# Output projection of a hybrid decoder block with seven products for eight, over pairs of token tiles

## The chip, the cores and the metric

The kernel runs on one core of a Trainium2 chip. The metric is the device time of one execution in microseconds. A core has TensorE (matmuls into the accumulators, PSUM), VectorE, ScalarE and GpSimd (shown as POOL), and SyncE, whose queue only sends transfers here. Transfers are sent from SyncE's queue (SP) or GpSimd's queue (POOL). A transfer that adds to what is at its destination goes through POOL.

## The reference

One layer over 2048 tokens of width 1024, float32:

```python
n = rms_norm(h, norm_w)
proj = jnp.einsum('bsd,de->bse', n, w_in)
pu, pz, q, k, v, dz, b, a = split(proj)
y_pool = pool_mixer(pu, pz, pool_w, pool_scale)
y_dn = deltanet_mixer(q, k, v, dz, b, a, conv_w, a_log, dt_bias, dn_norm_w)
y = jnp.concatenate([y_pool, y_dn], axis=-1)
h = h + jnp.einsum('bse,ed->bsd', y, w_out)     # the output projection
return rms_norm(h, final_norm_w)
```

The change concerns the last two lines: `y` (2048 x 1024) times `w_out` (1024 x 1024), the residual, and the norm of each token.

## The kernel before

The front of the kernel works in two blocks of 1024 tokens: the input projection, the pooling groups and the DeltaNet heads. Their results `y` are written to memory as `y_dram`, 16 tiles of 128 tokens, each tile held as 8 channel blocks of 128 (`KT` = 8).

Float32 products are made from three matmuls. A value is split into a part `hi` that TensorE's input type holds exactly and a rest `lo`; the product is `hi*hi + hi*lo + lo*hi`. A split is a copy on ScalarE (`hi`) and a subtraction on VectorE (`split_lo`, line 177).

The output stage, from line 836, goes over 16 token tiles and two halves of the 1024 outputs (`HALF` = 512). Per tile and half `out_mm` issues 8 channel blocks times three matmuls of 128 x 128 by 128 x 512 into one accumulator bank (24 matmuls). `load_wo` and `split_wo` bring and split `w_out`, in four pieces of two channel blocks per half, through the buffers `At`, `Ai`, `Tt` and `kT`, which the heads have left; `load_y` and `split_y` bring a `y` tile twice (`wh`, and `wl` by an adding transfer after ScalarE wrote the negative of `hi`). `load_res` brings the residual x into `kdec`. `out_add` adds the accumulator and x on VectorE and squares the sum on ScalarE; `out_norm` forms the norm's factor by 13 tiny VectorE operations, scales the tile and sends it out. The first two tiles are interleaved, (0, first half), (1, first half), (0, second), (1, second), because the second half of `w_out` needs the `nh`/`nl` buffers of the input projection.

The order of the work. Every function is entered by `at(slot, fn, ...)` with a time in slots, where one slot is one channel block, three matmuls. TensorE gets its instructions in exactly this order (`manual_schedule`, line 925). For the other engines and the queues the framework plans the order itself when the program is built: among what is ready it takes the earliest slot. Buffers belong to a tag with a number of copies (`st(shape, type, tag, copies)`); within a tag they are given out in the order of the slots, each as soon as a copy is free. On the chip each engine then works through its list in order.

In the code below, `slot` at line 900 is the slot at which the output stage starts on TensorE.

Of the kernel before, what the change touches and what calls it, by code (L numbers as in the profile page):

```python
# [19 lines left out]
NB = SEQ // TB  # L20
HALF = 512
# [56 lines left out]
def hymba_kernel(  # L78
# [18 lines left out]
    nc = tc.nc  # L97
# [9 lines left out]
    def st(shape, dt, tag, bufs=1):  # L107
        return sp.tile(shape, dt, tag=tag, name=tag, bufs=bufs)
# [8 lines left out]
    x0 = consts[:, C_X0:].rearrange("p (i c) -> p i c", i=COLS)  # L117
# [45 lines left out]
    y_dram = dp.tile([SEQ // P, P, KT, P], F32, tag="y_dram", name="y_dram")  # L163

    def rsqrt(y, v, shape):
        xh = st(shape, F32, "nr_x", 2)
        a = st(shape, F32, "nr_a", 2)
        nc.vector.tensor_scalar(
            out=y.bitcast(I32), in0=v.bitcast(I32), scalar1=-0.5, scalar2=MAGIC, op0=ALU.mult, op1=ALU.add
        )  # L170
        nc.vector.tensor_scalar(out=xh, in0=v, scalar1=-0.5, scalar2=None, op0=ALU.mult)
        for _ in range(3):
            nc.vector.tensor_tensor(out=a, in0=y, in1=y, op=ALU.mult)
            nc.vector.tensor_tensor(out=a, in0=a, in1=xh, op=ALU.mult)
            nc.vector.scalar_tensor_tensor(out=y, in0=a, scalar=1.5, in1=y, op0=ALU.add, op1=ALU.mult)

    def split_lo(eng, lo, full, hi):
        eng.tensor_tensor(out=lo, in0=full, in1=hi, op=ALU.subtract)
# [167 lines left out]
    def at(slot, fn, *args):  # L346
        events.append((slot, len(events), fn, args))
# [387 lines left out]
    slot = 0  # L735
# [3 lines left out]
    for b in range(NB):  # L739
# [12 lines left out]
        order = []  # L752
        i = 0
# [36 lines left out]
        for (kind, et, idx, res), hf in order:  # L790
# [7 lines left out]
            u = {"spare": 24 <= slot < 40}  # L798
# [34 lines left out]
        for h, res in heads:  # L833
            delta(b, h, res, gt, ends[h], ready)

    wo = {"hi": {}, "lo": {}}

    def load_wo(i, hf):
        wo["raw", i, hf] = wr = st([P, 2, HALF], F32, *((t := WO_TAGS[(4 * hf + i) % len(WO_TAGS)]), 2 if t == "kT" else 1))
        nc.sync.dma_start(wr, w_out[:, 2 * i : 2 * i + 2, hf * HALF : (hf + 1) * HALF])  # L840

    def split_wo(i, hf):
# [4 lines left out]
        nc.scalar.copy(wo["hi"][hf][:, ks], wo["raw", i, hf])  # L847
        split_lo(nc.vector, wo["lo"][hf][:, ks], wo["raw", i, hf], wo["hi"][hf][:, ks])

    def load_fw():  # L850
        wo["fw"] = fw = st([P, D], F32, "v0")
        nc.gpsimd.dma_start(fw, final_w[None, :].to_broadcast([P, D]))

    def load_y(ti, o):
        o["y"] = y_dram[ti]
        o["hi"] = st([P, KT, P], F32R, "wh", 3)
        o["lo"] = st([P, KT, P], F32R, "wl", 3)
        nc.gpsimd.dma_start(o["hi"], o["y"])
# [5 lines left out]
    def split_y(o):  # L864
        nc.scalar.activation(o["lo"], o["hi"].bitcast(F32), AF.Copy, scale=-1.0)
        nc.gpsimd.dma_start(o["lo"], o["y"], accum_op=ALU.add)

    def out_mm(o, hf, k):
        if k == 0:
# [3 lines left out]
        nc.tensor.matmul(ps, o["hi"][:, k], wo["lo"][hf][:, k], start=False, stop=False)  # L873
        nc.tensor.matmul(ps, o["lo"][:, k], wo["hi"][hf][:, k], start=False, stop=(k == KT - 1))  # L874

    def out_add(o, hf):
        if hf == 0:
            o["h"] = st([P, D], F32, "dec", 4)
            o["s2"] = st([P, 2], F32, "s2o", 2)
        dsl = slice(hf * HALF, (hf + 1) * HALF)  # L880
        nc.vector.tensor_tensor(out=o["h"][:, dsl], in0=o["ps", hf], in1=o["x"][:, dsl], op=ALU.add)  # L881
        junk = st([P, HALF], F32, "acc", 3)
        nc.scalar.activation(junk, o["h"][:, dsl], AF.Square, accum_out=o["s2"][:, hf : hf + 1])  # L883

    def out_norm(ti, o):
        ht, s2 = o["h"], o["s2"]
        v = st([P, 1], F32, "vo", 2)
        nc.vector.tensor_tensor(out=v, in0=s2[:, 0:1], in1=s2[:, 1:2], op=ALU.add)
        nc.vector.tensor_scalar(out=v, in0=v, scalar1=1.0 / D, scalar2=EPS, op0=ALU.mult, op1=ALU.add)
        r = st([P, 1], F32, "ro", 2)  # L890
        rsqrt(r, v, [P, 1])
        step = HALF if ti == SEQ // P - 1 else D
        for o0 in range(0, D, step):
            cs = slice(o0, o0 + step)
            nc.vector.scalar_tensor_tensor(
                out=ht[:, cs], in0=ht[:, cs], scalar=r[:, 0:1], in1=wo["fw"][:, cs], op0=ALU.mult, op1=ALU.mult
            )
            nc.sync.dma_start(out[ti * P : (ti + 1) * P, cs], ht[:, cs])

    for hf in range(NHALF):  # L900
# [5 lines left out]
    order = []  # L906
    for i in range(0, SEQ // P, 2):
        if i == 0:
            order += [(i, 0), (i + 1, 0), (i, 1), (i + 1, 1)]
        else:  # L910
            order += [(i, 0), (i, 1), (i + 1, 0), (i + 1, 1)]
    for ti, hf in order:
        o = outs[ti]
        if hf == 0:
            at(slot - 30, load_y, ti, o)
            at(slot - 20, load_res, ti, o)
            at(slot - 20, split_y, o)
        for k in range(KT):
            at(slot + k, out_mm, o, hf, k)
        slot += KT  # L920
        at(slot, out_add, o, hf)
        if hf == 1:
# [50 lines left out]
```

## Time and profile before

| | |
|---|---|
| times of three executions | 1006.13, 1009.9, 1010.2 us (median 1009.9) |
| time of the profiled execution | 1006.09 us |
| its span, first to last instruction | 1004.4 us |
| TensorE busy | 950.2 us, 95% |
| VectorE / ScalarE / GpSimd busy | 652.3 / 485.4 / 147.6 us |
| output stage, matmuls | 768, from 820.5 us |

The profile is of one execution. Times are microseconds from the start of the span unless marked ns. Busy time of TensorE counts overlapping matmuls once. In the groups, "out<-in" names the buffers, then come the shapes, the count, the busy time, the mean of one instruction in ns, and the idle time of the engine before them with what ended it. L872 is line 872. DVE is VectorE, ACT ScalarE, PEld TensorE's weight load, SPq and POOLq the queues.

### The profile page before, as it was taken

What the parts mean: (1) busy time and instruction counts of PE and PEld (TensorE: products, weight loads), DVE (VectorE), ACT (ScalarE), POOL (GpSimd) and SP (SyncE); (2) the same over time, 40 slices, a digit from 0 to 9 for tenths busy, and PEclk for the clock granted to TensorE, in tenths of its full rate; (3) what the DMA queues carried; (4) which work ended last, traced back from release to release, by engine and by line L of the source; (5) the groups of instructions that cost most, each with busy time, mean ns of one, the idle gap of its engine ahead of it and who ended that gap; (6) DMA issues with size and microseconds to landing.
All of it is one profiled execution on the core that took longest, in us unless ns stands there. A gap on an engine that the chain in (4) does not pass through costs nothing.

```text
span 1004.4 us, 14802 instructions
## 1 busy us (share of the span) xinstructions
PE 950.2 (95%) x5252; PEld 757.1 (75%) x5252; DVE 652.3 (65%) x2032; ACT 485.4 (48%) x1205; POOL 147.6 (15%) x200
## 2 busy tenths in 40 slices
PE   4989999989999999999899999999999999999996
PEld 3667777778777787767677777777778778888885
DVE  6676978668588355957886866858835483443343
ACT  7357665565564435516855455556443332222211
POOL 2214200101000014104410010101001101111100
PEclk9999999999999999999999999999999999999999
DMA  7431333332424346424242242242444576777761
GB/s 252 90 84 43 75 78 58 77 82 45 112 64 113 78 105 163 101 58 106 57 91 42 62 92 60 48 89 63 103 108 106 151 195 178 193 206 195 185 185 63
DMA packets 49434, 106.90 MB, mean 106 GB/s; under 512 B 4688, under 2 KB 22352, under 8 KB 49360
## 3 DMA queue, kind: packets, MB, share of 16 engines
q0 software_dynamic: 18000, 65.54, 30.4%
q1 hardware_dynamic: 31360, 40.41, 12.1%
q8 instruction: 41, 0.67, 0.3%
q14 instruction: 33, 0.27, 0.1%
HBM read 89.16 MB, written 16.78 MB: 105 GB/s over the span
## 4 chain that ended last, share of the span: by engine, by line
PE 56%; DVE 6%; issue 6%; DMA 4%; ACT 4%; POOL 0%; DVEq 0%; ACTq 0%; POOLq 0%
PE ps L375 10%; PE ps L377 9%; PE ps L376 9%; PE pso L874 6%; PE pso L873 6%; PE pso L872 6%; DMA wh<-in_w_in_dram 3%; PE ch L631 1%; PE tp L465 1%; DVE Ai L511 1%; PE qp L532 1%; PE ch L653 1%; PE ob L641 1%; PE ch L647 1%; PE ob L657 1%
## 5 line engine op out<-in xcount | busy, mean ns | idle before, releaser
L375 PE MATMUL ps<-nh,wh 128*128 128x512 f32 x768 | 335.6, 437 | 10.6 <-ACT nh L193 10.6
L377 PE MATMUL ps<-nh,wl 128*128 128x512 f32 x768 | 303.0, 395 | 1.8 <-DMA wl<-in_w_in_dram 1.8
L376 PE MATMUL ps<-nl,wh 128*128 128x512 f32 x768 | 302.3, 394 | 2.3 <-DVE nl L194 2.3
L375 PEld LDWEIGHTS ps<-nh,wh 128*128 128x128 f32 x768 | 145.9, 190 | 36.9 <-ACT nh L193 11.2
L377 PEld LDWEIGHTS ps<-nh,wl 128*128 128x128 f32 x768 | 145.0, 189 | 34.9 <-DMA wl<-in_w_in_dram 2.7
L376 PEld LDWEIGHTS ps<-nl,wh 128*128 128x128 f32 x768 | 146.1, 190 | 27.7 <-DVE nl L194 4.4
L389 DVE SCALAR_TENSOR_TENSOR acc<-u,cw,acc 128x512 f32<-128x512 f32 x144 | 112.5, 781 | 10.7 <-ACT acc L387 9.1
L872 PE MATMUL pso<-nh,wh 128*128 128x512 f32 x256 | 100.0, 391 | 0.0
L874 PE MATMUL pso<-nh,wl 128*128 128x512 f32 x256 | 99.7, 389 | 0.2 <-DMA wl<-y_dram 0.2
L873 PE MATMUL pso<-nl,wh 128*128 128x512 f32 x256 | 99.6, 389 | 0.0
L358 POOL DMA_DIRECT2D wh<-in_w_in_dram x46 | 26.6, 579 | 388.1 <-PE ps L377 375.0
L881 DVE TENSOR_TENSOR dec<-pso,kdec 128x512 f32<-128x512 f32 x32 | 22.1, 691 | 80.1 <-PE pso L874 80.1
L384 DVE TENSOR_TENSOR u<-ps,rb 128x512 f32<-128x512 f32 x48 | 33.1, 689 | 57.5 <-PE ps L377 57.3
L366 ACT ACTIVATE wl<-wh 128x1024 fp32r<-128x1024 f32 x46 | 48.8, 1061 | 44.0 <-DMA wh<-in_w_in_dram 35.2
L367 POOL DMA_DIRECT2D wl<-in_w_in_dram x46 | 39.7, 863 | 184.9 <-ACT wl L366 93.4
L883 ACT ACTIVATE acc<-dec 128x512 f32<-128x512 f32 x32 | 20.1, 629 | 85.3 <-DVE dec L881 85.3
L387 ACT ACTIVATE acc<-u,cw 128x512 f32<-128x512 f32 x48 | 34.6, 721 | 54.5 <-DVE u L384 52.4
L548 DVE TENSOR_TENSOR tmp<-Ai,X 128x60 f32<-128x60 f32 (+24 forms) x248 | 53.5, 216 | 4.0
L874 PEld LDWEIGHTS pso<-nh,wl 128*128 128x128 f32 x256 | 48.1, 188 | 10.6 <-DMA wl<-y_dram 0.6
L872 PEld LDWEIGHTS pso<-nh,wh 128*128 128x128 f32 x256 | 48.1, 188 | 10.2 <-ACT nh L847 0.2
L873 PEld LDWEIGHTS pso<-nl,wh 128*128 128x128 f32 x256 | 48.1, 188 | 10.0 <-issue 0.2
L554 DVE TENSOR_TENSOR X<-X,tmp 128x60 f32<-128x60 f32 (+24 forms) x248 | 52.5, 212 | 4.5
(214 smaller groups left out, 1511.4 us busy)
## 6 DMA issues: line engine op xcount, KB each, us to landing
wh<-in_w_in_dram POOLq DMA_DIRECT2D x46, 512.0 KB, 3.8
wl<-in_w_in_dram POOLq DMA_DIRECT2D x46, 512.0 KB, 5.6
y_dram<-yt SPq DMA_DIRECT2D x32, 256.0 KB, 3.1
kdec<-in_x_dram SPq DMA_DIRECT2D x16, 512.0 KB, 4.5
wh<-y_dram POOLq DMA_DIRECT2D x16, 512.0 KB, 4.0
wl<-y_dram POOLq DMA_DIRECT2D x16, 512.0 KB, 6.4
out_dram<-dec SPq DMA_DIRECT2D x15, 512.0 KB, 2.7
dec<-in_xT_dram SPq DMA_DIRECT2D x7, 512.0 KB, 7.8
```

Of the source, the lines that this page charges most:

```text
L366: nc.scalar.activation(w["lo"], w["hi"].bitcast(F32), AF.Copy, scale=-1.0)
L367: nc.gpsimd.dma_start(w["lo"], w_in[et], accum_op=ALU.add)
L375: nc.tensor.matmul(ps, w["hi"][:, k], nh[:, k], start=(k == 0), stop=False)
L376: nc.tensor.matmul(ps, w["hi"][:, k], nl[:, k], start=False, stop=False)
L377: nc.tensor.matmul(ps, w["lo"][:, k], nh[:, k], start=False, stop=(k == KT - 1))
L387: nc.scalar.activation(acc, ub[:, HALO:], AF.Copy, scale=cw[:, ci, CONV - 1 : CONV])
L389: nc.vector.scalar_tensor_tensor(out=acc, in0=ub[:, h0 + j : h0 + j + HALF], scalar=cw[:, ci, j : j + 1], in1=acc, op0=ALU.mult, op1=ALU.add,)
L548: nc.vector.tensor_tensor(out=tmp[:, 0:n, 0:w], in0=Ai[:, j, j + 1 : BS].unsqueeze(1).to_broadcast([P, n, w]), in1=X[:, 0:n, j : j + 1].to ...
L554: nc.vector.tensor_tensor(out=X[:, 0:n, j + 1 : BS], in0=X[:, 0:n, j + 1 : BS], in1=tmp[:, 0:n, 0:w], op=ALU.subtract)
L872: nc.tensor.matmul(ps, o["hi"][:, k], wo["hi"][hf][:, k], start=(k == 0), stop=False)
L873: nc.tensor.matmul(ps, o["hi"][:, k], wo["lo"][hf][:, k], start=False, stop=False)
L874: nc.tensor.matmul(ps, o["lo"][:, k], wo["hi"][hf][:, k], start=False, stop=(k == KT - 1))
```

## The change

Tiles 0 and 1 stay as they were, but with the second output half first. From tile 2 on two tiles form a pair, and the product of a pair is cut in two by tokens (the two tiles, rows 1 and 2 of A), by channels (blocks 0 to 3 and 4 to 7) and by outputs (the two halves, columns of B). Instead of eight products of these parts there are seven (Strassen's scheme in Winograd's form), each of 4 channel blocks x 3 matmuls, 12 for every product, 84 per pair for 96:

- sums of y: S1 = A21 + A22, S2 = S1 - A11, S3 = A11 - A21, S4 = A12 - S2
- sums of w_out, made once: T1 = B12 - B11, T2 = B22 - T1, T3 = B22 - B12, T4 = B21 - T2
- bank A takes A11 x B11, is copied out, takes S2 x T2 on top, is copied out, takes S3 x T3 on top, is copied out; bank B takes A12 x B21; bank C S1 x T1, is copied out, then S4 x B22 on top; bank D A22 x T4.

`pair_load` brings a pair's y once, unsplit (`r1` in the new tag `yr1` of two copies, `r21`, `r22`); `pair_a`, `pair_b`, `pair_c` form the sums on VectorE and split all operands, into `wh`/`wl` (three copies), `rb` and `acc`. `pair_seed` copies a bank to an output tile (`dec`) on ScalarE and adds x to it by an adding transfer from memory on POOL; `out_add` then adds the other bank. `t_load`, `t_sums` and `t_split` make the T matrices, one channel block k of four at a time: the raw parts B12 and B22 in `yr1`, B11 in `u`, B21 in `rb`; T1's split goes to `kT` and `qT`, T2's to `kdec` and `sz`, T3's to `At`, `Ai`, `Tt`, `vT`, and T4's over B12 in place, after the first two tiles' second half is done. The norms of both tiles of a pair come behind its last product. The last two tiles are written out in halves, before only the last one.

The diff, cut to its core:

```diff
-WO_TAGS = ("At", "Ai", "Tt", "kT")
+WO_TAGS = ("At", "Ai", "Tt", "vT")
+T_TAGS = {
+    "T1": (("kT", 2), ("kT", 2), ("qT", 2), ("qT", 2)),
+    "T2": (("kdec", 2), ("kdec", 2), ("sz", 2), ("sz", 2)),
+    "T3": (("At",), ("Ai",), ("Tt",), ("vT",)),
+}
...
+    def t_load(k, w):
+        w["bd"] = bd = st([P, 2, HALF], F32, "yr1", 2)
+        nc.sync.dma_start(bd, w_out[:, k : KT : NP, half(1)])
+        w["a"], w["c"] = st([P, HALF], F32, "u", 3), st([P, HALF], F32, "rb", 3)
+        nc.sync.dma_start(w["a"], w_out[:, k, half(0)])
+        nc.sync.dma_start(w["c"], w_out[:, k + NP, half(0)])
+
+    def t_sums(k, w):
+        a, b, c, d = w["a"], w["bd"][:, 0], w["c"], w["bd"][:, 1]
+        minus(a, b, a)
+        minus(b, d, b)
+        minus(d, d, a)
+        minus(c, c, d)
+        w.update(T1=a, T2=d, T3=b, T4=c)
+
+    def t_split(k, w, name):
+        if name == "T4":
+            hi, lo = wo["hi"][1][:, k], wo["lo"][1][:, k]
+        else:
+            if k % 2 == 0:
+                wo["t"][name, k // 2] = tuple(st([P, 2, HALF], F32R, *T_TAGS[name][2 * j + k // 2]) for j in range(2))
+            hi, lo = (t[:, k % 2] for t in wo["t"][name, k // 2])
+        nc.scalar.copy(hi, w[name])
+        split_lo(nc.vector, lo, w[name], hi)
...
     def load_res(ti, o):
-        o["x"] = xr = st([P, D], F32, "kdec", 2)
+        o["x"] = xr = st([P, D], F32, "dec", 4)
...
-        step = HALF if ti == SEQ // P - 1 else D
+        step = HALF if ti >= SEQ // P - 2 else D
...
+    def pair_load(t, q):
+        q["r1"] = st([P, KT, P], F32, "yr1", 2)
+        nc.sync.dma_start(q["r1"], y_dram[t])
+        for name, tag, lo in (("r21", "ps_s", 0), ("r22", "sacc", NP)):
+            q[name] = st([P, NP, P], F32, tag, 2)
+            nc.sync.dma_start(q[name], y_dram[t + 1][:, lo : lo + NP])
...
+    def pair_b(q):
+        two(q, "S2", "S1")
+        s1 = pair_sum(q, "S1", q["r21"], q["r22"], ALU.add)
+        s2 = pair_sum(q, "S2", s1, q["r1"][:, 0:NP], ALU.subtract)
+        pair_split(*q["S2"], s2)
+        pair_split(*q["S1"], s1)
...
+    BANKS = {"A": (pp, "pp"), "B": (pp, "pp"), "C": (pd, "pd"), "D": (pc, "pc")}
...
+    def pair_seed(q, bank, o, ti, hf):
+        if "h" not in o:
+            o["h"] = st([P, D], F32, "dec", 4)
+        nc.scalar.copy(o["h"][:, half(hf)], q[bank])
+        nc.gpsimd.dma_start(o["h"][:, half(hf)], x[ti * P : (ti + 1) * P, half(hf)], accum_op=ALU.add)
+
+    PRODUCTS = (
+        ("A", "A11", "B11", True),
+        ("B", "A12", "B21", True),
+        ("A", "S2", "T2", False),
+        ("C", "S1", "T1", True),
+        ("A", "S3", "T3", False),
+        ("D", "A22", "T4", True),
+        ("C", "S4", "B22", False),
+    )
...
-            at(slot - 22 + 16 * hf + 0.1 * i, load_wo, i, hf)
-            at(slot - 14 + 15 * hf + 3 * i, split_wo, i, hf)
+            at(slot - 22 + 16 * hf + 0.1 * i, load_wo, i, 1 - hf)
+            at(slot - 14 + 15 * hf + 3 * i, split_wo, i, 1 - hf)
+    for k in range(NP):
+        w = {}
+        at(slot - 3 + 4 * k, t_load, k, w)
+        at(slot + 4 + 4 * k, t_sums, k, w)
+        at(slot + 4.1 + 4 * k, t_split, k, w, "T2")
+        at(slot + 4.2 + 4 * k, t_split, k, w, "T1")
+        at(slot + 12.1 + 2 * k, t_split, k, w, "T4")
+        at(slot + 12.2 + 2 * k, t_split, k, w, "T3")
...
+    for t in range(2, SEQ // P, 2):
+        q, o1, o2 = {}, outs[t], outs[t + 1]
+        at(slot - 32, pair_load, t, q)
+        at(slot - 14, pair_a, q)
+        at(slot - 10, pair_b, q)
+        at(slot - 3, pair_c, q)
+        done = []
+        for bank, a, b, fresh in PRODUCTS:
+            for k in range(NP):
+                at(slot + k, pair_mm, q, bank, a, b, fresh, k)
+            slot += NP
+            done.append(slot)
+        at(done[0], pair_seed, q, "A", o1, t, 0)
+        at(done[2], pair_seed, q, "A", o1, t, 1)
+        at(done[3], pair_seed, q, "C", o2, t + 1, 1)
+        at(done[4], pair_seed, q, "A", o2, t + 1, 0)
+        add = lambda q, o, hf, bank: out_add(o, hf, q[bank], o["h"])
+        at(done[3] + 1, add, q, o1, 0, "B")
+        at(done[5] + 4, add, q, o2, 1, "A")
+        at(done[6], add, q, o2, 0, "D")
+        at(done[6] + 0.1, add, q, o1, 1, "C")
+        at(done[6] + 1, out_norm, t + 1, o2)
+        at(done[6] + 1.1, out_norm, t, o1)
```

More of the change, by code (lines that the diff above doesn't have):

```diff
@@ L874, in out_mm, with out_add @@
         nc.tensor.matmul(ps, o["lo"][:, k], wo["hi"][hf][:, k], start=False, stop=(k == KT - 1))
-    def out_add(o, hf):
-        if hf == 0:
+    def out_add(o, hf, ps, src):
+        if "h" not in o:
             o["h"] = st([P, D], F32, "dec", 4)
[L879 to L883, printed above, removed]
+        if "s2" not in o:
+            o["s2"] = st([P, 2], F32, "s2o", 4)
+        nc.vector.tensor_tensor(out=o["h"][:, half(hf)], in0=ps, in1=src[:, half(hf)], op=ALU.add)
+        junk = st([P, HALF], F32, "t11")
+        nc.scalar.activation(junk, o["h"][:, half(hf)], AF.Square, accum_out=o["s2"][:, hf : hf + 1])
     def out_norm(ti, o):
@@ new lines, in pair_mm @@
+    def pair_mm(q, bank, a, b, fresh, k):
+        if fresh and k == 0:
+            pool, tag = BANKS[bank]
+            q[bank] = pool.tile([P, HALF], F32, tag=tag, name="ps" + bank)
+        ps = q[bank]
+        (ah, al), (bh, bl) = (t[:, k] for t in q[a]), w_part(b, k)
+        args = dict(skip_group_check=True)
+        nc.tensor.matmul(ps, ah, bh, start=(fresh and k == 0), stop=False, **args)
+        nc.tensor.matmul(ps, ah, bl, start=False, stop=False, **args)
+        nc.tensor.matmul(ps, al, bh, start=False, stop=(k == NP - 1), **args)
```

64 lines of the change are left out of this document (47 added, 17 removed).

## The prediction

> **What bounds the kernel now.** I read the page's first block, then the table of windows over the last stage, then TensorE's order of time there, its groups by line and its waits. First the page's span and busy time, and three windows (columns: stretch, length, then busy time with count of TensorE, its weight load, VectorE, ScalarE, GpSimd; granted clock, DMA share, GB/s).
>
> ```profile
> span 1004.4 us, 14802 instructions
> PE 950.2 (95%) x5252; PEld 757.1 (75%) x5252; DVE 652.3 (65%) x2032; ACT 485.4 (48%) x1205; POOL 147.6 (15%) x200
> 820.00:842.40 22.40, 22.24 (x96) 17.74 (x96) 10.13 (x23) 8.70 (x14) 2.88 (x4) 1.00 0.52 127
> 952.10:974.00 21.90, 21.90 (x99) 18.12 (x98) 9.20 (x32) 5.02 (x10) 2.83 (x4) 1.00 0.69 195
> 996.10:1004.40 8.30, 0.00 (x0) 0.00 (x0) 4.05 (x16) 0.72 (x2) 0.00 (x0) 0.71 0.17 64
> ```
>
> In a window of two token tiles (952 to 974) TensorE is busy for all of it, VectorE for 9.20 of 21.90 us. The first and last matmul of the output projection, the three groups, and the only wait on a TensorE matmul there:
>
> ```profile
> 820.50 0.39 PE L872 MATMUL pso<-nh,wh 128*128 128x512 f32 x1
> 995.70 0.39 PE L874 MATMUL pso<-nh,wl 128*128 128x512 f32 x1
> L872 PE MATMUL pso<-nh,wh 128*128 128x512 f32 x256 | 100.0, 391 | 0.0
> L874 PE MATMUL pso<-nh,wl 128*128 128x512 f32 x256 | 99.7, 389 | 0.2 <-DMA wl<-y_dram 0.2
> L873 PE MATMUL pso<-nl,wh 128*128 128x512 f32 x256 | 99.6, 389 | 0.0
> PE pso L874 <- DMA wl<-y_dram: 0.2, 1, 0.2
> ```
>
> The mean of 390 ns overlaps its neighbours; what counts is the step. 16 pieces of 48 matmuls are 768 in 820.50 to 995.93, 228 ns each; in the undisturbed part four of the 24-matmul products take 21.76 us, 0.2267 us a matmul. So this stage costs what its count of matmuls costs. I write a slot for one k step, three matmuls, 0.68 us; slot 0 is 820.5.
>
> **The change, part by part.**
>
> *Matmuls.* Each of 7 pairs goes from 4 x 8 x 3 = 96 matmuls to 7 x 4 x 3 = 84. 7 x 12 x 0.2267 = 19.0 us less, all on the path. The shapes do not change, so neither does the step.
>
> *Prices on VectorE and ScalarE* (groups by line, then order of time):
>
> ```profile
> L881 DVE TENSOR_TENSOR dec<-pso,kdec 128x512 f32<-128x512 f32 x32 | 22.1, 691 | 80.1 <-PE pso L874 80.1
> L883 ACT ACTIVATE acc<-dec 128x512 f32<-128x512 f32 x32 | 20.1, 629 | 85.3 <-DVE dec L881 85.3
> 806.65 2.17 DVE L420 TENSOR_TENSOR ps_s<-ps_s 128x525 f32<-128x525 f32 x3
> 826.16 1.22 DVE L178 TENSOR_TENSOR nl<-kT,nh 128x1024 fp32r<-128x1024 f32 x1
> 827.29 0.75 DVE L440 SCALAR_TENSOR_TENSOR yt<-pm,psc,szp 128x512 f32<-128x512 f32 x1
> 827.96 0.68 DVE L881 TENSOR_TENSOR dec<-pso,kdec 128x512 f32<-128x512 f32 x1
> 839.85 0.16 DVE L888 TENSOR_TENSOR vo<-s2o 128x1 f32<-128x1 f32 x1 [0.79 <-ACT acc L883]
> 842.17 1.28 DVE L895 SCALAR_TENSOR_TENSOR dec<-dec,ro,v 128x1024 f32<-128x1024 f32 x1
> 843.81 0.69 DVE L881 TENSOR_TENSOR dec<-pso,kdec 128x512 f32<-128x512 f32 x1 [0.36 <-PE pso L874]
> ```
>
> From start to start VectorE takes 0.67 us for 128x512 (827.29 to 827.96), 0.72 when each needs the last (2.17 for three), 1.13 for 128x1024 (826.16 to 827.29), and 3.6 for a tile's norm (839.85 to 843.81 less 0.36). ScalarE takes 0.63 for 512.
>
> *A pair in steady state.* VectorE: the split of A11/A12 1.13; four sums and five splits 9 x 0.67 = 6.0; four adds 2.7; two norms 7.2; together 17.0 us in a pair that TensorE now does in 84 x 0.2267 = 19.0. ScalarE: 1.1 + 5 + 4 copies and 4 squares of 0.63 with 0.2 each for the sums, some 10 us. Both fit, so I price them at nothing; the cover is TensorE's 19.0 us, and the margin on VectorE is 2.0. Without it each microsecond over 19.0 costs a microsecond a pair. The operands have time: A11/A12's buffer comes free 20 slots (13.6 us) before the next pair needs it, S2/S1's and S3/A22's likewise. POOL loses the two y DMAs per tile and gets four quarter-megabyte accumulating ones per pair; SP gets three loads per pair for two. Bytes fall: y with its second, accumulating read and x for two tiles were 3 MB, now 1 MB of y and 1 MB of accumulation. The seeds are not needed for 4 to 16 slots (2.7 to 11 us):
>
> ```profile
> wl<-y_dram POOLq DMA_DIRECT2D x16, 512.0 KB, 6.4
> kT<-in_w_out_dram SPq DMA_DIRECT2D x2, 512.0 KB, 4.3
> 718.34 0.37 SPq L840 DMA_DIRECT2D kT<-in_w_out_dram  x1
> ```
>
> Accumulating 512 KB took 6.4 us to land; half as much is bounded by 3 (half) and 6.4, I take 4.5. The tightest add (o2, output half 1) has 4 slots before A is even complete, so VectorE's wait there lies between 0 and 1.8 us a pair, inside its margin: 0 taken.
>
> *The T matrices, once.* Four channel blocks k, each a load of 512 KB (b and d) and two of 256 KB, four sums and four splits: 4 x 8 x 0.67 = 21.5 us on VectorE, 16 x 0.63 = 10 on ScalarE. This is where the gain is lost. The loads come as early as their buffers allow: the row at 718.34 is a w_out load a hundred us ahead of its use, sent when kT came free. But yr1 has two buffers, handed out in the order of the events: k=0, then pair 1's r1 (slot 0, held until its last sum), then k=1 (slot 1), k=2, k=3. So k=1, 2, 3 pass one after another through one buffer, each waiting until the one before has split T2 and T3 out of it. T3 of k=0 goes into At and Tt, which hold the raw w_out half until its split. Before, the splits of the second half ended at 827.3 (the fence above); with k=0's T1 and T2 among them (1.3), the yt and out_add rows behind (1.4) and T4 and T3 themselves (1.3), k=0 lets go at about 831. A round is 4.3 for the load, 2.7 for sums, 2.7 for splits, 0.3 between engines: 10.0. k=1 lets go at 841, k=2 at 851; k=3 lands at 855.3, its T2 is there after three sums and the split on both engines, 855.3 + 2.1 + 0.63 + 0.67 + 0.1 = 858.8. TensorE wants S2 x T2 at k=3 in slot 32 + 8 + 3 = 43, 849.7. Wait: 9.1 us. Bounds: nothing, if k=1 to 3 could be loaded ahead; 12 with rounds of 11. I take 9, as each part has its row. Behind it T1, T3, T4 of k=3 follow at 0.67 us while each product takes 2.72, so no second wait. From 820.5 to 859 VectorE has 4.6 of old splits, 1.4 of pools, 21.5 for T, 5.6 for three adds and a norm, and some 6 of pair 1's own sums and splits: 39 us in 38, just full; what spills over is owed only two products later. Between 0 and 3, 0.5 taken.
>
> *The restart after it.* TensorE then stands idle for some 7 us. What that does at the kernel's start:
>
> ```profile
> 9.75 0.80 PE L375 MATMUL ps<-nh,wh 128*128 128x512 f32 x1 [9.75 <-ACT nh L193]
> 11.13 0.63 PE L377 MATMUL ps<-nh,wl 128*128 128x512 f32 x1
> 12.84 0.51 PE L375 MATMUL ps<-nh,wh 128*128 128x512 f32 x1
> 13.19 0.40 PE L376 MATMUL ps<-nl,wh 128*128 128x512 f32 x1
> 17.16 0.50 PE L376 MATMUL ps<-nl,wh 128*128 128x512 f32 x1 [1.34 <-DVE nl L194]
> 17.50 0.40 PE L377 MATMUL ps<-nh,wl 128*128 128x512 f32 x1
> ```
>
> After 9.75 us of idleness seven matmuls took 9.75 to 13.19, 3.44 us for 1.59; after 1.34 us none was slow for more than its own fill. So the wait costs 1.85 more: 1.8, bounds 0 (the idleness comes in short pieces) and 1.85. [...]
>
> *The tail.* Rows of the end:
>
> ```profile
> 996.13 0.69 DVE L881 TENSOR_TENSOR dec<-pso,kdec 128x512 f32<-128x512 f32 x1 [4.75 <-PE pso L874]
> 999.99 1.42 DVE L895 SCALAR_TENSOR_TENSOR dec<-dec,ro,v 128x512 f32<-128x512 f32 x2
> 1000.77 1.00 SPq L898 DMA_DIRECT2D out_dram<-dec  x2
> ```
>
> From the last add to the end 8.3 us. In the new order the second tile's last product (A22 x T4) ends only 2.72 us before the last, so about 2.5 of its 3.6 us norm stands in the way of the other tile's: +2.2, bounds 0 (it fits into the wait for the square) and 3.6.
>
> *First four products.* Halves swapped and x in dec for kdec: order and count stay, 0. Their y loads now meet the pair's loads; the 0.2 us wait on y could become 1, 0.2 taken.
>
> Sum: -19.0 + 9.1 + 0.5 + 1.8 + 2.2 + 0.2 = -5.2 us. The profiled execution took 1006.09 (span 1004.4), so 1000.9 against its own time. The three times are 1006.13, 1009.9 and 1010.2; the profiled one lies 3.8 under their median, and -5.2 from the median is 1004.7. Midway: 1002.8.
>
> **The rivals.**
>
> *All of T is hidden.* For: VectorE's 65% over the span leaves room earlier, and the loads are small. Against: the single yr1 buffer and At/Tt, both bound to slot 10 or later. No wait, no restart: -19.0 + 2.2 + 0.7 = -16.1, 990 against the profiled run, 994 against the median.
>
> *VectorE becomes the bound.* 17.0 of 19.0 is 89%, in an order fixed beforehand; if waits for ScalarE's copies and for seeds leave it idle 3.3 us a pair, a pair takes 20.3, and 7 x 1.3 = 9 us of the gain go as well: 1009.9 against the profiled run, 1013.8 against the median at that size; at half of it 1005 to 1009, no difference. For: 95% of VectorE's time from 820 on would be filled. Against: its deadlines are 13 us wide.
>
> *The A bank turns round too slowly* (the other sign). A holds P1, then S2 x T2 and S3 x T3 on top; ScalarE has to copy it out between, within 4 slots, 2.72 us, of which the copy takes 0.63 and hand-overs some 0.3. If ScalarE stands at a copy that waits for a VectorE sum behind a 3.6 us norm, it comes 3.6 - 1.8 = 1.8 late. 14 such turns: from a mean of 5.2 / 14 = 0.37 us nothing is gained, from 0.73 the kernel is 0.5% slower; at 1.8 us it is 1026. For: the wait has no buffer to dodge to. Against: before, ScalarE is busy 5.02 of 21.90 us in the stage and reached its work within 0.1 us of release.
>
> *The matmuls do not run at the old step* because stationary operands change places: nothing in the weight-load row (18.12 of 21.90 busy) speaks for it.
>
> **How the numbers follow.** Forecast (a wait of 5 to 11 us at pair 1, the rest hidden) 0.52, giving 997 to 1007; hidden T 0.15; VectorE bound 0.18; A bank 0.13; other 0.02. 0.5% of 1009.9 is 5.0 us, about what a measurement here can tell from no change. Faster takes all of hidden T, 0.37 of the forecast's 0.52 and little of the third: 0.54. Same: 0.14 of the forecast, 0.12 of VectorE, 0.04: 0.30. Slower: 0.16. The range 992 to 1011 takes in both readings of the base and half of the two neighbours.
>
> **What would show it.** 96 + 7 x 84 = 684 matmuls in the stage at 0.2267 us; a wait of 7 to 10 us ahead of the third product of pair 1, on VectorE's T2 split, with slow matmuls behind it; w_out loads of 512 KB spaced by 10 us from about 831; VectorE at 85 to 95% in a pair's window; a tail of 10 to 11 us. Wrong would be: T loads close together, waits of TensorE on ScalarE's copies out of PSUM at each pair, or a pair's window over 19.5 us.

## The result and the profile after

The changed kernel took 1022.85 us (median; 1019.07 to 1025.98), the kernel before 1009.97 in the same comparison: ratio 1.0135 [1.0086, 1.0184]. It is slower, by some 13 us, where 7 us faster was forecast. The profiled execution took 1025.98 us. First its page, then three windows of the output stage and one of the end; the columns are those of the prediction's tables.

```profile
span 1024.3 us, 14882 instructions
PE 946.8 (92%) x5168; PEld 747.9 (73%) x5168; DVE 706.3 (69%) x2135; ACT 520.0 (51%) x1277; POOL 151.6 (15%) x200
```

```profile
825.05:854.28 29.23, 24.67 (x99) 19.32 (x99) 24.56 (x42) 14.13 (x23) 0.88 (x1) 0.94 0.53 164
854.28:886.66 32.38, 21.66 (x85) 17.02 (x84) 24.11 (x53) 12.45 (x24) 3.45 (x4) 0.84 0.56 155
927.86:949.58 21.72, 19.68 (x85) 15.61 (x84) 14.29 (x43) 8.45 (x18) 3.40 (x4) 1.00 0.59 147
1012.30:1024.30 12.00, 0.00 (x0) 0.00 (x0) 7.14 (x32) 1.44 (x4) 0.00 (x0) 0.70 0.23 87
```

The 84 matmuls fewer are there: 5168 for 5252. But TensorE, busy for all of a window before, now has holes: 4.6 us in the first four products (first row), 10.7 in pair 1 (second row), 2.0 in a later pair (third row). The waits of TensorE's matmuls from 800 us on (engine, accumulator, line, what released it: total us, times, longest us):

```profile
PE psA L995 <- ACT dec L1002: 7.9, 10, 1.3
PE psA L995 <- ACT kdec L882: 7.4, 1, 7.4
PE pm L443 <- DVE acc L437: 4.6, 1, 4.6
PE psA L996 <- DVE sz L183: 3.4, 1, 3.4
```

Before, this list held one wait of 0.2 us in the output products. Now there are three places: the T2 split at pair 1 (rows 2 and 4), the last pooling product `pm`, which stands among the first four products (row 3), and ten waits on ScalarE's copy out of bank A (row 1).

**How the stages are compared.** The moment at which the output stage starts on TensorE lay between 818.07 and 830.58 us in the profiles of all kernels below. It goes with the clock granted to TensorE until then: over 0 to 407 us this was 1.00 in five profiles (both of the kernel before, seeds without x, both left out, and both additions to the first combination), which start at 818.07 to 820.50, and 0.97 to 0.99 in the nine others, which start at 823.20 to 830.58. Whether the edits have a part in that was not tested, so the stage is measured by its own length: from its first output matmul to the end of the span. The pieces are from first matmul to first matmul: the first four products, then each pair. Each row is one profile; a second profile of the kernel before gave a stage length 0.5 us from the first.

| kernel | first four | pair 1 | pairs 2 to 7 | tail | stage |
|---|---|---|---|---|---|
| before | 23.1 | 21.8 | 6 x 21.77 | 8.3 | 183.9 |
| changed | 29.2 | 32.4 | 19.7 to 21.7 | 12.0 | 199.3 |
| seeds without x | 28.5 | 32.2 | 19.1 to 19.3 | 9.8 | 185.4 |
| no T matrices | 24.6 | 19.2 | 19.8 to 22.4 | 11.6 | 181.1 |
| both left out | 25.0 | 19.0 | 19.0 to 19.2 | 9.6 | 168.0 |
| pair 1's raw y later | 35.5 | 19.1 | 19.8 to 21.9 | 11.8 | 191.2 |
| pooling product later | 27.4 | 32.5 | 19.6 to 22.2 | 12.2 | 197.3 |
| x loaded ahead | 29.6 | 31.9 | 19.1 to 19.3 | 9.9 | 186.3 |
| squares behind the copies | 29.4 | 32.5 | 19.1 to 20.7 | 12.3 | 190.9 |
| first combination | 31.3 | 20.0 | 22.8, then 19.1 to 19.3 | 9.9 | 179.7 |

Against before the changed stage is 15.4 us longer: 7 x 84 matmuls at 0.2267 us in place of 7 x 96 give -19.0; the first four products +6.1; pair 1, 32.4 against 19.04, +13.3; pairs 2 to 7, 125.64 against 6 x 19.04, +11.4; the tail +3.7. The experiments show two causes behind these four losses: the T work (first four products and pair 1) and the adding transfers of the seeds (pairs 2 to 7 and the tail).

**The chain at pair 1.** TensorE, SyncE's queue, ScalarE and VectorE in order of time (start, us, queue or engine, line, operation, out<-in; in brackets the idle time before and its releaser):

```profile
837.25 0.56 SPq L861 DMA_DIRECT2D yr<-in_w_out_dram  x1
847.32 10.37 SPq L861 DMA_DIRECT2D yr<-in_w_out_dram  x2
868.61 0.62 ACT L882 CAST kdec<-yr 128x512 fp32r<-128x512 f32 x1 [0.48 <-DVE yr L868]
869.28 0.80 PE L995 MATMUL psA<-kdec,wh 128*128 128x512 f32 x1 [7.36 <-ACT kdec L882]
872.70 0.69 DVE L183 TENSOR_TENSOR sz<-yr,kdec 128x512 fp32r<-128x512 f32 x1
873.44 0.79 PE L996 MATMUL psA<-sz,wh 128*128 128x512 f32 x1 [3.36 <-DVE sz L183]
876.59 0.61 PE L997 MATMUL psC<-kT,wl 128*128 128x512 f32 x1
877.02 0.43 PE L995 MATMUL psC<-kT,wh 128*128 128x512 f32 x1
```

The loads of blocks k=1, 2 and 3 leave ten microseconds apart (837.25, 847.32, and the second of the pair at about 857.1), as the prediction had them, and k=3 can be summed from 861.1 on. But the hi part of T2 for k=3 arrives only at 869.2, and TensorE has waited 7.36; the lo part is late too, at 873.4. In between VectorE does other sums and splits that stand ahead of these in its list, and waits 2.2 us for a seed's transfer. From 869.28 to 877 the matmuls step at 0.43 us.

**The chain at the first four products.** VectorE and TensorE:

```profile
816.09 0.69 DVE L868 TENSOR_TENSOR u<-yr,u 128x512 f32<-128x512 f32 x1 [2.12 <-DMA u<-in_w_out_dram]
...
831.87 0.69 DVE L437 SCALAR_TENSOR_TENSOR acc<-ps_s,u 128x512 f32<-128x512 f32 x1
832.62 1.19 PE L443 MATMUL pm<-acc,pw 128*128 128x512 f32 x1 [4.56 <-DVE acc L437]
```

The first T sum stands at the head of VectorE's list and waits 2.12 us for its load; four sums and two splits of k=0 (some 4 us) then lie ahead of the last pooling group's mix, L437, on which TensorE waits.

**The turn of bank A in a steady pair.** Rows of the pair that begins at 927.86:

```profile
934.50 0.85 POOL L1003 DMA_DIRECT2D dec<-in_x_dram  x1 [10.16 <-ACT dec L1002]
939.20 0.69 DVE L915 TENSOR_TENSOR dec<-psB,dec 128x512 f32<-128x512 f32 x1 [1.64 <-issue]
939.98 0.63 ACT L917 ACTIVATE t<-dec 128x512 f32<-128x512 f32 x1 [4.83 <-DVE dec L915]
940.61 0.56 ACT L1002 COPY dec<-psA 128x512 f32<-128x512 f32 x1
941.23 0.50 PE L995 MATMUL psA<-At,wh 128*128 128x512 f32 x1 [1.24 <-ACT dec L1002]
```

S2 x T2 starts at 934.26 and its 12 matmuls are done about 937.0, but ScalarE copies bank A only at 940.61: it has stood 4.83 us at the square of a sum that VectorE could not form, and behind that copy S3 x T3 waits. The ten waits of this kind add up to 7.9 us. The rest of the 11.4 is some 0.35 us behind each, until the matmuls step at 0.2267 again. What VectorE waited for is not named in this row; over the stage the lists say it:

```profile
ACT t L917 <- DVE dec L915: 66.3, 17, 6.0
```

```profile
DVE dec L915 <- DMA dec<-in_x_dram: 39.4, 15, 7.9
```

```profile
dec<-in_x_dram POOLq DMA_DIRECT2D x28, 256.0 KB, 5.8
```

So: the seed's adding transfer takes 5.8 us to land (third fence, median), the add stands before it on VectorE, the square stands before the next copy on ScalarE, and TensorE needs that copy. The tail has the same two transfers in it:

```profile
1010.39 0.69 DVE L915 TENSOR_TENSOR dec<-psA,dec 128x512 f32<-128x512 f32 x1 [7.91 <-DMA dec<-in_x_dram]
1012.49 0.69 DVE L915 TENSOR_TENSOR dec<-psD,dec 128x512 f32<-128x512 f32 x1 [1.40 <-DMA dec<-in_x_dram]
```

### The profile page after: what moved, and what is told of

It reads as the page before. It is cut to its first block, busy times and chain, and to the rows that moved or that the text cites. A ratio compares the mean times of both kernels' runs of the same rounds, so it can differ in the third digit from the quotient of the medians.

```text
span 1024.3 us, 14882 instructions
## 1 busy us (share of the span) xinstructions
PE 946.8 (92%) x5168; PEld 747.9 (73%) x5168; DVE 706.3 (69%) x2135; ACT 520.0 (51%) x1277; POOL 151.6 (15%) x200
## 5 line engine op out<-in xcount | busy, mean ns | idle before, releaser
L381 PEld LDWEIGHTS ps<-nl,wh 128*128 128x128 f32 x768 | 147.4, 192 | 27.4 <-issue 4.3
L372 POOL DMA_DIRECT2D wl<-in_w_in_dram x46 | 39.4, 856 | 189.2 <-ACT wl L371 100.3
L392 ACT ACTIVATE acc<-u,cw 128x512 f32<-128x512 f32 x48 | 34.6, 721 | 54.5 <-DVE u L389 52.4
L917 ACT ACTIVATE t<-dec 128x512 f32<-128x512 f32 x32 | 20.2, 631 | 72.0 <-DVE dec L915 66.3
L1003 POOL DMA_DIRECT2D dec<-in_x_dram x28 | 23.9, 865 | 157.2 <-ACT dec L1002 148.1
L477 ACT ACTIVATE sqj<-tp 128x128 f32<-128x128 f32 x128 | 34.1, 277 | 14.9 <-PE tp L470 14.9
L665 ACT ACTIVATE sqj<-v 128x128 f32<-128x128 f32 x64 | 19.5, 305 | 37.4 <-DVE v L663 31.4
L636 PEld LDWEIGHTS ch<-state,kT 128*128 128x128 f32 x128 | 21.4, 188 | 21.6 <-DVE state L659 19.0
L654 ACT ACTIVATE nv<-ch,sm 128x128 f32<-128x128 f32 x64 | 23.4, 366 | 23.5 <-PE ch L652 23.5
L638 DVE SCALAR_TENSOR_TENSOR rho<-ch,negc,v 128x128 f32<-128x128 f32 x64 | 22.3, 349 | 17.9 <-PE ch L636 17.4
L636 PE MATMUL ch<-state,kT 128*128 128x128 f32 x128 | 27.6, 297 | 7.7 <-DVE state L659 7.1
```

The source lines that it names most:

```text
L372: nc.gpsimd.dma_start(w["lo"], w_in[et], accum_op=ALU.add)
L381: nc.tensor.matmul(ps, w["hi"][:, k], nl[:, k], start=False, stop=False)
L392: nc.scalar.activation(acc, ub[:, HALO:], AF.Copy, scale=cw[:, ci, CONV - 1 : CONV])
L477: nc.scalar.activation(junk, tp[:, j], AF.Square, accum_out=dst[:, c : c + 1])
L636: nc.tensor.matmul(ch[:, 0], res["kT"][:, t], S, start=True, stop=True)
L1003: nc.gpsimd.dma_start(o["h"][:, half(hf)], x[ti * P : (ti + 1) * P, half(hf)], accum_op=ALU.add)
```

## The experiments

**Seeds without x.** The adding transfers out of the changed kernel; the copies, adds and squares stay.

```diff
         nc.scalar.copy(o["h"][:, half(hf)], q[bank])
-        nc.gpsimd.dma_start(o["h"][:, half(hf)], x[ti * P : (ti + 1) * P, half(hf)], accum_op=ALU.add)
```

> The changed kernel without the transfers that add x to the seeds of the pairs (the residual of tiles 2 to 15 is left out). Theory (seed transfer): an add on VectorE stands waiting for x to land, its square keeps ScalarE, and behind the square waits the copy that clears bank A. Then the waits ahead of the S2 x T2 and S3 x T3 products from pair 2 on, 11.2 us in all, go to under 2, and the tail from the last matmul goes from 12.1 to about 9.5: 12 to 14 us faster than the changed kernel, 1009 to 1011. Rival (VectorE's load of 17 of 19 us makes the copy late, not the landing): the instructions on VectorE and ScalarE are the same, so the waits stay, within 3 us of the changed kernel.

Measured: 1009.08 us, ratio to before 1.0012 [0.9995, 1.003]. The window of one pair, and what TensorE still waited for in the stage:

```profile
879.64:898.76 19.12, 19.12 (x86) 15.77 (x85) 14.29 (x43) 8.96 (x18) 0.00 (x0) 1.00 0.30 110
```

```profile
PE psA L995 <- ACT kdec L882: 6.2, 1, 6.2
PE pm L443 <- DVE acc L437: 4.0, 1, 4.0
PE psA L996 <- DVE sz L183: 3.3, 1, 3.3
```

The ten waits on bank A are gone and each pair takes 84 steps and no more, with the same 43 VectorE and 18 ScalarE instructions. VectorE is busy 14.3 us of 19.1, so its load was not the bound of a steady pair. The stage is 13.9 us shorter: 10.8 in pairs 2 to 7 and 2.2 in the tail, the rest in the first four products and pair 1.

**No T matrices.** No T loads, sums or splits; the products take the plain parts of w_out in their place.

```diff
     def w_part(name, k):
-        if name == "T4":
...
+        name = {"T1": "B12", "T2": "B22", "T3": "B22", "T4": "B21"}.get(name, name)
...
-    for k in range(NP):
+    for k in ():
```

> The changed kernel without the T matrices: no loads, sums and splits for them, the products take plain parts of w_out instead. Theory: the wait of the pooling product before the stage (4.6 us and 2 of slow matmuls) and the loss of pair 1 (13.3 us) both come from the T work: 18 to 20 us faster than the changed kernel, 1003 to 1005. Rival (pair 1 waits for its own sums and splits of y, late on a full VectorE): 8 to 12 us faster, with a wait of TensorE in pair 1 left.

Measured: 1006.8 us, ratio 0.9973 [0.9955, 0.9991]. The waits of the stage:

```profile
PE psA L991 <- ACT dec L998: 8.3, 10, 1.9
```

One more wait, of 1.7 us, is at tile 1's y. Pair 1 takes 19.2, the first four products 24.6. So the T work costs 4.6 of the 6.1 us at the first four products as well as all of pair 1's 13.3; ten A-bank waits stay, as they have another cause.

**Both left out**, the two edits above together.

> The changed kernel without the T work and without x in the pairs (tiles 2 to 15 get neither; the products take plain parts of w_out): what the fewer matmuls are worth by themselves. Theory: 84 matmuls fewer at 0.2267 us and nothing else but the longer tail, a stage of 166 to 169 us against 183.9: 14 to 18 us faster than before. Rival (a further cost of the pairs that the two others covered): 5 to 12 us.

Measured: 991.75 us, ratio 0.9832 [0.9798, 0.9866]. The first four products and pair 1:

```profile
818.49:843.50 25.01, 22.95 (x100) 18.32 (x98) 16.19 (x30) 10.18 (x17) 0.88 (x1) 1.00 0.39 108
843.50:862.54 19.04, 19.04 (x86) 15.77 (x84) 15.46 (x35) 9.88 (x20) 0.00 (x0) 1.00 0.31 111
```

This is what the seven products are worth by themselves: 16.9 us by the two times of the kernels (15.9 by the stage), near the -19.0 of the prediction less a longer tail and a wait of 2.1 us for tile 1's y. The two causes add up to within 0.8 us: the stage shortens by 13.9 without the seeds' transfers, by 18.1 without T, and by 31.2 (for 32.0) without both.

**x loaded ahead.** All of the work is kept. x goes into the output tile by a plain transfer before the pair, ScalarE copies the bank to a buffer, and GpSimd adds it.

```diff
-        nc.scalar.copy(o["h"][:, half(hf)], q[bank])
-        nc.gpsimd.dma_start(o["h"][:, half(hf)], x[ti * P : (ti + 1) * P, half(hf)], accum_op=ALU.add)
+        c = st([P, HALF], F32, "yt", 2)
+        nc.scalar.copy(c, q[bank])
+        h = o["h"][:, half(hf)]
+        nc.gpsimd.tensor_tensor(out=h, in0=h, in1=c, op=ALU.add)
+
+    def pair_x(ti, o):
+        o["h"] = st([P, D], F32, "dec", 4)
+        nc.sync.dma_start(o["h"], x[ti * P : (ti + 1) * P, :])
...
+        at(slot - 12, pair_x, t, o1)
+        at(slot - 12, pair_x, t + 1, o2)
```

> x is loaded into the output tile ahead, the bank is copied to a small tile by ScalarE, and GpSimd adds it to x on chip (1.4 us by the profile's 128x512 add) in place of the transfer that adds x. All results are kept. Theory (seed transfer): as without x at all, 10 to 14 us faster than the changed kernel. Rival (order and load of VectorE and ScalarE): 0 to 4 us.

Measured: 1011.11 us, ratio 1.004 [1.0018, 1.0062]. The stage is 13.0 us shorter than the changed kernel's, nearly as without x, and the three waits left are the T work's (6.2, 4.5, 3.4). It is the transfer in the middle of the chain that costs, not the addition of x.

**Squares behind the copies.** The adding transfers stay as they are; on ScalarE the square of a sum is placed behind the next copy out of a bank, and the norms a little later.

```diff
+        if behind and seeds:
+            with tc.issue_after(seeds[-1]):
+                return out_sq(o, hf)
...
-        at(done[6] + 1, out_norm, t + 1, o2)
-        at(done[6] + 1.1, out_norm, t, o1)
+        last = t == SEQ // P - 2
+        at(done[3] + 1.1, out_sq, o1, 0, True)
+        sq = done[6] + (0.5 if last else 4.05)
+        at(sq, out_sq, o2, 1, True)
...
```

> The changed kernel with the squares of a pair queued on ScalarE behind the seed copy that stands next in time; transfers, sums and splits are kept. Theory (a square behind an add that waits for its seed's transfer keeps ScalarE from clearing bank A): of the 11.2 us of waits from pair 2 on 6 to 10 go, what is left comes from the hi copies that wait for VectorE, itself at the same transfer; 5 to 9 us faster. Rival (the landing reaches bank A by another way, or the copy itself is slow): 0 to 2 us.

Measured: 1014.91 us, ratio 1.008 [1.0055, 1.0106]; the stage 8.3 us shorter than the changed kernel's. VectorE's and TensorE's waits (the line numbers moved by 9):

```profile
DVE dec L915 <- DMA dec<-in_x_dram: 34.6, 18, 5.1
```

```profile
PE psA L1004 <- ACT kdec L882: 6.7, 1, 6.7
PE pm L443 <- DVE acc L437: 3.9, 1, 3.9
PE psA L1005 <- DVE sz L183: 3.4, 1, 3.4
PE psA L1004 <- ACT dec L1011: 1.3, 1, 1.3
```

VectorE waits for the transfers almost as long as before (34.6 for 39.4 us), and the ten A-bank waits have become one: pairs 2 to 7 lose 2.5 us for 11.4. So in these pairs 8.9 of the 11.4 us come from the slow landing by way of the square's place in ScalarE's list. The edit moves the norms a little as well; what share that has was not measured apart. The tail keeps its loss (12.3 us).

**Pair 1's raw y later.** It asks for its buffer behind the T blocks instead of between them.

```diff
-        at(slot - 32, pair_load, t, q)
+        at(slot - (20 if t == 2 else 32), pair_load, t, q)
```

> The first pair's y load (r1) is entered behind the four T loads, so that the T loads have both buffers of yr1 and r1 comes after. Theory (one buffer in a row): two rounds of 10 us fall away, pair 1's loss of 13.3 us goes to 3 to 5, 8 to 10 us faster than the changed kernel. Rival (VectorE is full in the first 35 us, the buffer does not matter): 0 to 3 us.

Measured: 1017.58 us, ratio 1.0083 [1.0051, 1.0116]. The long waits of the stage:

```profile
840.69 2.07 PE L443 MATMUL pm<-acc,pw 128*128 128x512 f32 x2 [10.19 <-DVE acc L437]
```

Pair 1 is clean (19.1 us): T2's last split, for k=3, is now done 26.9 us after the stage's start, in place of 48.4 in the changed kernel. TensorE came to it at 36.7 there, so there would have been no wait even without the longer first four products; the single buffer was the cause there. But the T blocks now come earlier on VectorE, ahead of the last pooling group, and the wait at `pm` grew from 4.56 to 10.19. Of the 13.3 us at pair 1, 6.3 came back at the first four products.

**The last pooling product later**, by 12 slots.

```diff
-                at(te + L_POOL, lambda u=u, b=b, idx=idx, hf=hf, res=res: pool_out(u, b, idx, hf, res))
+                at(te + L_POOL + (12 if (b, idx, hf) == (NB - 1, GROUPS - 1, 1) else 0), lambda u=u, b=b, idx=idx, hf=hf, res=res: pool_out(u, b, idx, hf, res))
```

> The changed kernel with the last pooling product entered 12 slots later on TensorE, so that TensorE no longer stands at it while VectorE is behind. The 4.6 us wait and the slow matmuls after it go from the first four products (29.2 to about 23.5 us). Theory (the row of T loads through one buffer runs on its own clock, not TensorE's): pair 1 then waits that much longer for T2, so only 0 to 2 us are gained. Rival (the losses add up independently): 6 us faster than the changed kernel.

Measured: 1023.66 us, ratio 1.0161 [1.0131, 1.0191]: in time nothing gained that is clear of noise, in the stage 2.0 us. The two longest waits are now

```profile
836.24 0.50 PE L908 MATMUL pso<-nh,wl 128*128 128x512 f32 x1 [2.81 <-DMA wl<-y_dram]
872.19 0.80 PE L995 MATMUL psA<-kdec,wh 128*128 128x512 f32 x1 [8.75 <-ACT kdec L882]
```

The wait at `pm` is gone. A wait of 2.81 us at tile 1's y, with slow matmuls behind it, took its place, so that the first four products gain 1.8 us only. Pair 1 keeps its loss (32.5): T2's hi part arrives 44.9 us after the stage's start, for 44.2 in the changed kernel, so TensorE waits longer there.

**First combination**: x loaded ahead, pair 1's raw y later and the pooling product later, the three edits above together.

> Three edits together, all results kept: x loaded ahead and added on GpSimd, the first pair's y entered behind the T loads, the last pooling product 12 slots later. Theory (the three losses found are all there is): 23 to 24 us for the first four products, 19.1 for every pair, a tail of 10, so a stage of 167 to 169 us against 183.9 before: 13 to 17 us faster than before, 992 to 996. Rival (VectorE cannot make T, the splits and the pools in the first 25 us): a wait of 4 us or more of TensorE before pair 2, 6 to 12 us faster than before.

Measured: 1003.49 us, ratio 0.9962 [0.9943, 0.9982]: faster than both kernels, by about 4 us against before, much less than was expected; by stages 179.7 against 183.9. Its longest waits:

```profile
PE pso L908 <- DMA wl<-y_dram: 4.4, 1, 4.4
PE psA L995 <- ACT yt L1001: 1.8, 1, 1.8
```

From pair 3 on the pairs take 19.1 us. The first four products and pairs 1 and 2 (windows):

```profile
825.85:857.11 31.26, 25.46 (x100) 19.79 (x99) 27.36 (x44) 15.88 (x26) 0.88 (x1) 0.89 0.57 174
857.11:877.08 19.97, 19.44 (x86) 15.71 (x85) 19.97 (x43) 10.45 (x20) 8.71 (x4) 1.00 0.48 155
877.08:899.89 22.81, 21.05 (x85) 16.86 (x84) 21.97 (x51) 9.06 (x20) 6.09 (x4) 0.93 0.65 230
```

Of the 15.9 us by which the stage shrinks with both left out, some 11.6 are lost again, nearly all of it in these three rows (31.3, 20.0 and 22.8 for 25.0, 19.0 and 19.0), where VectorE is busy 27.36 of 31.26 us, then all of 19.97. Not all of that is work: some VectorE operations take longer beside GpSimd's additions, 1.27 us for at most 0.16 (last section). Pair 2 has the wait of 1.8 us at `yt` and slow matmuls behind it.

**T sums on GpSimd** (added to the first combination), and **tile 1's y out of the buffers `wh` and `wl`** (added to the first combination):

```diff
-        minus = lambda o, x0, x1: nc.vector.tensor_tensor(out=o, in0=x0, in1=x1, op=ALU.subtract)
+        minus = lambda o, x0, x1: nc.gpsimd.tensor_tensor(out=o, in0=x0, in1=x1, op=ALU.subtract)
```

> The same with the four sums of each T block on GpSimd (1.43 us each by the profile) in place of VectorE, so that VectorE does not stand at a T load. If VectorE's place in the first 25 us is what is left, 2 to 4 us faster than without; if nothing is left, equal; if GpSimd's four sums of 5.7 us a block come too late for T2 (wanted some 30 us after the stage's start), slower by 1 to 5.

```diff
-        o["hi"] = st([P, KT, P], F32R, "wh", 3)
-        o["lo"] = st([P, KT, P], F32R, "wl", 3)
+        o["hi"] = st([P, KT, P], F32R, *(("kdec", 2) if ti else ("wh", 3)))
+        o["lo"] = st([P, KT, P], F32R, *(("sz", 2) if ti else ("wl", 3)))
```

The second edit was meant to give tile 1's y buffers of its own. But `kdec` and `sz` are the buffers of T2's two parts, two copies each, so y now shares them with T2.

> The version with three edits (x ahead and added on GpSimd, first y behind the T loads, last pooling product later), and tile 1's y in kdec and sz, which are free 30 us before the stage, in place of wh and wl. Theory (its wait of 4.4 us was tile 1's second y transfer, sent only when wl came free and slowed by the w_out loads beside it): the wait goes, first four products 24 to 27 us, 4 to 7 us faster than with three edits: 10 to 12 us faster than before. Rival (VectorE is behind by then, the wait moves to the pooling product or to pair 1): 0 to 3 us faster than with three edits.

Measured: 1008.63 us, ratio 1.0012 [0.9995, 1.0029], stage 183.7; and 1011.7, 1.0039 [1.0015, 1.0064], stage 186.2. Neither helps. The first has its longest wait at tile 1's y, the second at pair 1's own operand:

```profile
PE pso L908 <- DMA wl<-y_dram: 8.2, 1, 8.2
```

```profile
860.59 1.14 ACT L882 CAST kdec<-yr 128x512 fp32r<-128x512 f32 x2 [2.15 <-PE pso L907]
870.00 0.80 PE L995 MATMUL psA<-nh,wh 128*128 128x512 f32 x1 [9.22 <-ACT wh L942]
```

In the first GpSimd's sums stand in its list ahead of the y transfers that it sends. In the second y's wait is gone, and others of 4.29 (`pm`) and 9.22 us have come. The row at 860.59 shows why: T2's split of k=2 and 3 could start only when tile 1's last product had let go of `kdec`; pair 1's raw y was sent behind it, at 863.33. So this run does not test what y in buffers of its own would give. Of the first, the expectation of a small loss came (5 us against the first combination); the second missed both of its forecasts.

**Both added to the first combination.**

> This is the fourth of the combined versions: x loaded ahead into the output tile and the seed added on GpSimd, the chain of the T loads relieved by loading pair 1's raw y later, the last pooling product 12 slots later, tile 1's y in kdec and sz, and the 16 sums for the T matrices on GpSimd in place of VectorE. It takes 16 x 0.67 = 10.7 us off VectorE around the stage's start, and tile 1's y no longer waits for a buffer. Theory (VectorE is simply full there, so each wait removed came back as another until work was taken off it): first four products about 25 us, pair 1 about 20, the other pairs 19.1, the stage 171 to 176 us, some 3 to 8 us faster than the version with x ahead and the two reorderings (1003.5), so 996 to 1001. Rival (the place where a sum is made does not matter, since GpSimd takes 1.3 to 3.4 us for one and the chain of loads, sums and splits of four blocks through few buffers is then the longer one, 4 x 4 sums of 1.4 to 2.0 = 22 to 32 us): TensorE waits at pair 1 or 2 for a T split for 5 us or more, the stage is 180 us or longer, 1003 us or more.

Measured: 1013.78 us, ratio 1.0079 [1.0054, 1.0104], stage 189.5. Pair 1's raw y is sent, and TensorE starts pair 1, at

```profile
854.20 0.33 SPq L936 DMA_DIRECT2D yr<-y_dram  x1
861.34 0.79 PE L995 MATMUL psA<-nh,wh 128*128 128x512 f32 x1 [15.88 <-ACT wh L942]
```

Taking 10.7 us of work off VectorE did not shorten the start, and the times that the rival gave came out, but not the place that it named: the wait is at pair 1's own operand and not at a T split. In order: the w_out loads of k=2 and 3 leave at 834.8, their sums on GpSimd take 1.3 to 1.7 us each and last until 851.0, T2's splits follow on VectorE at 853.4 and 855.2, and pair 1's y is sent between them, at 854.2. This kernel also has T2's buffers shared with tile 1's y, so the runs do not separate the slow sums, the shared buffers and the order of the lists. That "VectorE is full" was too simple is shown; that the T blocks' passage through loads, sums and splits in few buffers limits the start is argued from these rows and not shown.

**The kernel before once more**, for the stage's start.

> The kernel before, profiled once more, to see how far the start of the output stage and its length move from run to run. If the 4.55 us by which the stage began later in the changed kernel's profile is chance, the stage starts anywhere between 819 and 828 here too and is again 183.5 to 184.5 long; if the change did it, 820.5 within 1 us.

Measured: stage from 818.07, 184.4 us long, against 820.50 and 183.9. The stage's length repeats within 0.5 us, its start less well (2.4 us apart, both at a granted clock of 1.00 over the first 407 us).

## Why the prediction was wrong

*Matmuls, -19.0:* right. 0.2267 us a step; 84 steps in 19.04 us where nothing waits.

*The T wait, 9.1, and the clock's restart, 1.8:* the mechanism is right: the 10 us rounds through one buffer are in the trace (loads at 837.25, 847.32 and about 857.1; the 0.3 "between engines" in each was an estimate of mine), and without them (pair 1's raw y later) the wait is gone. That the size is near is partly luck. TensorE came to T2 36.7 us after the stage's start, where 29.2 was forecast, as the first four products were longer; T2 was whole at 48.4 where 38.3 was forecast. The two errors partly cancel. The step that failed is the price of "three sums and the split" behind the landing of k=3, 3.5 us: from the first sum to the hi part it took 8.1, to the lo part 12.3, since VectorE's list had other work in between. So the lo part came 3.36 us after the hi part, a second wait at the same product. The restart was paid once: the granted clock was 0.50 from 869.28 to 877.02, through the second wait, and the nine slow steps cost 1.5 us. 13.3 in place of 11.4 (9.1 + 0.5 + 1.8): 10.7 of waits, 1.5 of slow steps and about 1 more, of which the matmul at 869.28, alone between the two waits, is 0.57 (0.80 us for a step of 0.2267).

*Steady pairs, "Both fit, so I price them at nothing" and "VectorE's wait there lies between 0 and 1.8 us a pair, inside its margin: 0 taken":* this is the main step that failed, +11.4 us. VectorE's own 17.0 us a pair was even too high (14.3 measured). But the wait, 39.4 us in seven pairs or 5.6 a pair, was no idleness inside a margin: the add waits for a transfer, ScalarE's square for the add, the copy of bank A for the square. The sum of busy times looked at each engine alone. The rival "The A bank turns round too slowly" named the place and the threshold: 11.4 us over the 12 turns of pairs 2 to 7 is 0.95 us each, above its 0.73. Its cause was another, a transfer in place of a sum behind a norm; seeds without x and squares behind the copies show that. Two of the prediction's own signs came with it: waits on ScalarE's copies, and pairs longer than 19.5 us.

*The seed's landing, 4.5 us taken from 3 to 6.4:* 5.8 in the median. Half the bytes came 0.6 us sooner than the 6.4 of the kernel before, under another load. The deadline that I compared it with, "not needed for 4 to 16 slots", is that of the tile. The tile could wait; VectorE, which takes its list in order, could not.

*First four products, 0.2:* +6.1. I costed only the y loads and left out that T's sums and splits of k=0 come into VectorE's list ahead of the last pooling group. Without T this piece took 24.6 and 25.0, so T is 4 to 5 of it and tile 1's y 1.7 to 2.1.

*The tail, 2.2:* 3.7, as two adds wait for transfers there; without the transfers 9.8 or 9.9 us, +1.5.

*VectorE at 85 to 95% in a pair's window:* wrong, 14.29 of 21.72 us is 66%. All of T hidden, and VectorE as the bound of a pair: both out, by the T waits and by that row.

*The sum:* by its terms it is -5.2 us. The 7 us below the measured median of the kernel before come of the step that put its time midway between the profiled time and the median; no mechanism stands behind the other 1.8.

## What to carry to other kernels

Add up engines' busy times to see whether work fits, but then follow the order inside each list: an instruction that waits for a transfer held up everything behind it on its engine here (VectorE's adds waited 39.4 us for transfers, ScalarE's squares 66.3 for the adds, TensorE 7.9 at ten copies behind the squares), so a wait that is harmless to its own tile can travel over two engines to an accumulator bank. When one buffer's turn is needed within a few slots, put nothing in front of its copy that depends on a transfer; moving the square behind the copy recovered 8.9 of the 11.4 us lost in pairs 2 to 7, with the transfers as slow as they were. And when a removed wait comes back elsewhere, look for the resource that the steps share before moving the next one: three changes here (pair 1's raw y later, the pooling product later, tile 1's y in other buffers) cleared one wait each and raised another, the last because the buffers were those of T2.

## What the runs showed of the hardware

*Landing time of an adding transfer.* In the changed kernel 28 of 256 KB (`dec<-in_x_dram`) landed in 5.8 us (median; 4.0 to 7.3), and 46 of 512 KB (`wl<-in_w_in`, an earlier stage) in 5.6 (5.3 to 8.4); in the kernel before, 16 of 512 KB (`wl<-y_dram`) in 6.4. So the size does not show in these medians, but the load around the transfers differs. How much of a landing does not depend on size no run here isolates.

*When matmuls become slow.* After the wait of 4.56 us the granted clock was 0.52 for 3.5 us (832.62 to 836.14), after that of 7.36 us 0.50 from 869.28 through the second wait to 877.02. The length of the wait does not decide here: matmuls were slow after waits of 1.76 us (first combination, 884.45; clock 0.52, seven steps of 0.42 to 0.43 us from the fifth on), 2.58 (T sums on GpSimd, 831.38; 0.50, one matmul of 0.77 us before the next wait) and 2.81 (pooling product later, 836.24; 0.55, eight steps of 0.39 to 0.43 us from the second on), and not after 1.85 (no T matrices, 941.38; 1.00), 2.06 (both left out, 827.50; 1.00) and 3.58 (both added, 834.31; 1.00), where the steps behind the first are 0.22 to 0.24 us. What else the clock's fall depends on stays open.

*GpSimd's 128x512 addition beside a busy VectorE.* In the first combination, all 28 of them (min/median/max ns):

```profile
L1003 POOL TENSOR_TENSOR dec<-dec,yt x28: 1287/1418/3439, 861.6 to 990.9; 128x512 f32<-128x512 f32 x28
```

One takes 1.3 to 3.4 us. Some of VectorE's operations beside them are longer as well:

```profile
861.55 3.44 POOL L1003 TENSOR_TENSOR dec<-dec,yt 128x512 f32<-128x512 f32 x1 [32.87 <-ACT yt L1001]
863.75 1.27 DVE L178 TENSOR_TENSOR nr_a<-ro 128x1 f32<-128x1 f32 x1
```

In the changed kernel this small operation of L178 took at most 0.16 us. No run here isolated what makes either of them longer.
